# The first down-projection of a transformer block as seven products of quarters, with the context's feed-forward in a phase of its own

## The chip, the cores and the metric

The kernel runs on one core of a Trainium2 chip. A core has a matrix engine (TensorE, called PE in the profile), three engines that work on rows of 128 partitions (VectorE or DVE, ScalarE or ACT, GpSimd or POOL) and a queue (SyncE or SP) that issues the transfers between HBM and the on-chip memory SBUF. PE writes its results to eight accumulation banks of 128 x 512 floats (PSUM), from which ACT or DVE must carry them away. The metric is the time of one execution on the device, in microseconds (us), as the median of several runs.

## The reference, cut to what matters

One layer of a diffusion trunk over 1024 latent tokens and 256 context tokens, 1024 channels each, all in float32. Only the first half of the layer matters here:

```python
def _swiglu(h, w1, w3, w2):
    return (jax.nn.silu(h @ w1) * (h @ w3)) @ w2       # w1, w3: 1024 x 2816, w2: 2816 x 1024

x     = _residual(x,     _swiglu(_modnorm(x,     g[0], m[0],  m[1]),  w1, w3, w2), g[1], m[2],  0.5)
h_ctx = _residual(h_ctx, _swiglu(_modnorm(h_ctx, g[0], mc[0], mc[1]), w1, w3, w2), g[1], mc[2], 0.5)
...   # then projections of both, two attentions, a merge, and a second feed-forward for x alone
def _residual(x, y, g_post, gate, weight):
    return x + weight * gate * _rmsnorm(y, g_post)
```

The product with `w1` and `w3` is the up-projection, the one with `w2` the down-projection. `m` and `mc` are rows of modulation, made from a conditioning vector by nine products with `w_ada`.

## The kernel before, in words

**Three products for one.** PE multiplies float32 numbers that are rounded to a shorter form. To keep the precision every operand is split into a high part (ACT copies it in the short form) and a low part (DVE subtracts the copy from the original); `split` does this, and `mm3` then issues three products: high x high, high x low, low x high.

**Products of quarters.** The up-projection of the latent tokens already saves products: the operands are cut into quarters, and seven products of sums of quarters stand for eight products of quarters. `Unit` is one such set of products for 256 columns of a weight, and makes its sums of weight quarters on DVE. The second feed-forward does the same in its down-projection. There `Gated` stores the gated up-projection (`silu(h w1) * (h w3)`) as seven matrices, three quarters and four sums (`s1` to `s4`, four DVE operations and four stores more for each of the 11 pairs of weight columns, `sums`), and `Quarters` runs 7 x 11 = 77 steps: step n loads one 128 x 512 piece of a matrix (`load_a`, seven steps ahead), splits it and a piece of a weight quarter or of a sum of them (`split`, three steps ahead), and issues four groups of three products into four banks (`product`). The sums of weight quarters (`t1` to `t4`, 44 DVE operations) are made in place by `sum` at steps that `plan` sets. After every eleventh step DVE or ACT takes the four banks out (`out`). The second, third, fifth, sixth and seventh set of eleven steps either go on in the banks of the set ahead, so that PE must not write a bank before it has been read, or start in others.

**The first down-projection is plain.** `Down` takes the 22 row blocks of `w2` in ten groups (nine of two, one of four). For every group it computes ten tiles of 128 tokens x 1024 channels, 0 to 7 the latent tokens, 8 and 9 the context, in two halves, and adds them to `ys` with DVE. Between these tiles stand 44 steps `ctx_up`, the context's up-projection (24 products of 256 columns each). The gated context halves stay in SBUF and enter tiles 8 and 9 as further rows of the same group, with the same split weights.

**The order of the work** is written out by hand. `Plan.step` appends a step of PE work, `Plan.spread` hangs side work (loads, splits, sums) on step numbers, `run` issues step after step. Each engine and the SP queue then works in just this order (`keep_in_program_order`): an instruction that waits holds all behind it. A load of the plan goes into SP's queue at its step; a store, two steps after it was asked for.

**The tail of the phase.** When a tile of `ys` is done, `residual_steps` makes the residual: load of `x` one step ahead (`zero`); at the next step the root of the mean square (ACT squares, POOL takes the power) and, on DVE, a scaling and an addition of 128 x 1024 (`one`, `two`); two and four steps later a second root and a scaling on ACT (`three`, `four`). `plan_chains` puts these at the steps of `pos`. `fill0` then transposes the first four tiles on PE and splits them into the planes for the next projections, whose first product follows at once.

The second down-projection ends in another form of this, `done2`: at its steps 55, 57, 59 and 61 the load of a tile of `x` and a scaling, one step later the addition on DVE and at once (`store(..., 0)`) the store to the output, so that in SP's queue the next tile's load stands behind this store.

**Side work in the same stretch**: `ada_steps(...)` are the modulation products; for each of them DVE adds up 16 scaled pieces of a matrix, or 32 where the context needs its own row (m below 5).

**Buffers**: SBUF pools of 24 tiles `u` and 16 tiles `v` of 128 x 1024, 20 tiles `t` of 128 x 512; PSUM banks `s` (3), `m` (3), `v` (2). The profile names tiles `xu`, `xv`, `t`, `bs`, `bm`, `bv` and all scratch in HBM `d`. Products have line L154 (`mmul`), transposes L157 (`turn_`), all of ACT, DVE and POOL outside attention L120, transfers L132.

Of the kernel before, what the change touches and what calls it, by code (L numbers as in the profile page):

```python
# [43 lines left out]
def hybrid_block(ctx: ExitStack, tc: tile.TileContext, a: dict, out: bass.AP):  # L44
# [25 lines left out]
    def V(dt=F32):  # L70
        return U(dt, "v")
# [313 lines left out]
    def gate_rows(col, key="u"):  # L385
        row = U(key=key)
        for h in range(2):
            pb = PB("s")
# [345 lines left out]
    def up_units(h, w1, w3, gd):  # L734
# [3 lines left out]
        def pair_(p):  # L738
# [6 lines left out]
            def emit3(i, ci, x, bank):  # L745
                y = s.pop((i, ci))
                vec.tensor_tensor(y, x, y, op=ALU.mult)
                if isinstance(gd, Gated):
                    gd.put(p, i, ci, y, units[2 * p + 1].led)
                else:  # L750
                    store(gd[2 * p + i, :, ci * 512:(ci + 1) * 512], y)
# [7 lines left out]

    lap = [0]  # L760

    def PD():
        lap[0] = (lap[0] + 1) % 8
        return PB("smvsmvsm"[lap[0]])

    class Down:


        def __init__(self, w2, gd, ys, fs):
            self.w2, self.gd, self.ys, self.fs = w2, gd, ys, fs  # L770
            self.w, self.g, self.c, self.r = {}, {}, {}, {}

        def loads(self, f, key="v"):
            self.r[f] = load(self.w2[f], key=key), load(self.gd[f], key=key)

        def steps(self, fs=None, key="v"):

            fs = fs or self.fs

            def one(f, e):  # L780
                self.w.setdefault(f, []).append(split(self.r[f][0][:, e * 512:(e + 1) * 512]))

            def two(f):
                self.g[f] = split2(self.r.pop(f)[1])

            s = []
            for f, after in zip(fs, fs[1:] + [None]):
                s += [lambda f=f: one(f, 0), lambda f=f: one(f, 1), lambda f=f: two(f)]
                if after is not None:
                    s[-2] = lambda f=f, n=after: (one(f, 1), self.loads(n, key))  # L790
            return s

        def tile(self, t, es=range(2)):
            ys, fs = self.ys, self.fs
            g = self.g if t < 8 else self.c
            c = slice((t % 8) * P, (t % 8 + 1) * P)
            if fs[0] == 0 and 0 in es:
                ys[t] = V()
            for e in es:
                o = slice(e * 512, (e + 1) * 512)  # L800
                pd = PD()
# [357 lines left out]
    for d in downs:  # L1159
        d.c = cc  # L1160
# [1173 lines left out]
```

## Time and profile before

| what | value |
|---|---|
| median of three runs | 2609.99 us (2607.43 to 2613.73) |
| the profiled execution | 2611.61 us, its span 2609.8 us |
| PE busy | 2576.4 us (99%), 13596 products and transposes |
| DVE, ACT, POOL busy | 1869.2 us (72%), 1189.7 us (46%), 229.4 us (9%) |
| transfers | 433.30 MB, 166 GB/s over the span |
| granted PE clock | 0.997 of full speed |

The span is the time from the first to the last instruction; the execution's own time has 1.8 us more around it. The stages follow each other on PE: up-projection of the latent tokens from 19 to about 455 us, the first down-projection with the context's feed-forward to about 894 us, the projections, the attentions, and from 1871 us the second feed-forward, whose down-projection (in quarters) starts at about 2386 us. In the timelines below the first two columns are the start and the length of a merged group in us, "x6" counts its instructions, and brackets hold the idle time of that engine ahead of the group and what ended it. Instructions of one engine overlap a little: the distance from start to start tells what one costs, not its length.

### The profile page before, as it was taken

Reading aid. Unit: us, or ns where it says so; the run is one execution under the profiler, and the core shown is the slowest. Engines: PE = TensorE matmul, PEld = TensorE weight load, DVE = VectorE, ACT = ScalarE, POOL = GpSimd, SP = SyncE. Lnnn points to the kernel's source line nnn. Section 1 sums busy time; section 2 is a strip of 40 time slices with the busy share of each in tenths; the row PEclk is TensorE's granted clock in tenths of the full one; section 3 lists DMA queues with packets and bytes.
Section 4 is the critical chain, followed back from the end, with each engine's and each line's share of the span. In section 5 each row is a group of like instructions: output and inputs, shape, how many; then the busy total and the mean of one; then the engine's idle time right before and its main releaser. Section 6 shows DMA issues by size and latency. Waiting matters only on the chain.

```text
span 2609.8 us, 37912 instructions
## 1 busy us (share of the span) xinstructions
PE 2576.4 (99%) x13596; PEld 2194.1 (84%) x13596; DVE 1869.2 (72%) x3536; ACT 1189.7 (46%) x2282; POOL 229.4 (9%) x368
## 2 busy tenths in 40 slices
PE   8999999999999999999999999999999999999998
PEld 6888888888888788889889999997788888888886
DVE  4778876587776676775468988886635788766777
ACT  6622223532223663434348987773246322323444
POOL 1000000000000400001003522221021000000003
PEclk9999999999999999999999999999999999999999
DMA  8444433454443575655987742206325444326714
GB/s 303 165 160 142 146 120 117 149 178 149 155 141 114 194 248 175 232 170 173 283 308 268 248 100 74 69 9 223 121 98 192 149 159 167 114 97 239 264 55 174
DMA packets 213501, 433.30 MB, mean 166 GB/s; under 512 B 26880, under 2 KB 68032, under 8 KB 213312
## 3 DMA queue, kind: packets, MB, share of 16 engines
q1 hardware_dynamic: 213312, 430.87, 49.5%
q8 instruction: 107, 1.75, 0.3%
q14 instruction: 82, 0.67, 0.1%
HBM read 318.78 MB, written 112.00 MB: 165 GB/s over the span
## 4 chain that ended last, share of the span: by engine, by line
PE 55%; issue 32%; DVE 6%; ACT 4%; DMA 1%; POOL 1%; SPq 0%; DVEq 0%; ACTq 0%; POOLq 0%
PE bs L154 24%; PE bm L154 16%; PE bv L154 12%; PE bm L157 2%; ACT xu L1914 1%; DVE xu L1778 1%; DVE xv L120 1%; DVE t L1941 1%; ACT t L1940 1%; DVE xu L120 1%; PE bs L157 1%; DVE t L120 1%; POOL st L120 1%; ACT t L1914 0%; ACT t L1754 0%
## 5 line engine op out<-in xcount | busy, mean ns | idle before, releaser
L154 PE MATMUL bm<-xu,xu 128*128 128x512 f32 (+1 forms) x1980 | 469.6, 388 | 1.1 <-ACT t L120 0.8
L154 PEld LDWEIGHTS bm<-xu,xu 128*128 128x128 f32 x1980 | 363.4, 188 | 74.5 <-ACT t L120 2.1
L154 PE MATMUL bs<-xv,xu 128*128 128x512 f32 x1488 | 357.3, 389 | 0.3 <-DVE t L120 0.3
L154 PE MATMUL bv<-xv,xu 128*128 128x512 f32 x1342 | 335.4, 389 | 0.0
L154 PE MATMUL bs<-xu,xu 128*128 128x512 f32 (+1 forms) x1404 | 334.0, 384 | 0.0
L154 PEld LDWEIGHTS bs<-xv,xu 128*128 128x128 f32 x1488 | 279.2, 188 | 58.5 <-issue 0.7
L120 ACT CAST xu<-t 128x512 fp32r<-128x512 f32 x260 | 158.2, 616 | 356.3 <-DVE t L120 355.6
L154 PEld LDWEIGHTS bs<-xu,xu 128*128 128x128 f32 x1404 | 258.0, 188 | 52.0 <-issue 0.8
L154 PEld LDWEIGHTS bv<-xv,xu 128*128 128x128 f32 x1342 | 251.9, 188 | 52.3
L120 DVE TENSOR_TENSOR xu<-t,xu 128x512 fp32r<-128x512 f32 x260 | 178.6, 688 | 127.2 <-ACT xu L120 127.2
L120 DVE TENSOR_TENSOR xu<-xu,xu 128x512 fp32r<-128x512 f32 (+2 forms) x245 | 168.5, 692 | 66.2 <-ACT xu L120 64.6
L120 POOL TENSOR_SCALAR st<-st 128x1 f32<-128x1 f32 (+1 forms) x66 | 42.1, 638 | 1928.0 <-ACT t L120 1917.5
L154 PE MATMUL bs<-w,w 96*128 96x512 f32 (+3 forms) x832 | 206.8, 367 | 2.4 <-DVE st L1803 1.9
L120 DVE TENSOR_TENSOR xu<-xv,xu 128x512 fp32r<-128x512 f32 (+4 forms) x196 | 141.3, 743 | 42.0 <-ACT xu L120 38.8
L154 PE MATMUL bm<-t,xu 128*128 128x256 f32 (+1 forms) x1272 | 165.3, 287 | 0.6 <-ACT t L120 0.4
L154 PEld LDWEIGHTS bm<-t,xu 128*128 128x128 f32 x1272 | 160.7, 191 | 6.0 <-ACT t L120 0.8
L120 ACT ACTIVATE t<-t 128x512 f32<-128x512 f32 (+1 forms) x94 | 57.3, 610 | 223.2 <-DVE t L120 214.2
L120 DVE TENSOR_TENSOR t<-t,t 128x512 f32<-128x512 f32 (+2 forms) x196 | 125.2, 639 | 45.6 <-ACT t L120 42.0
L154 PE MATMUL bv<-t,w 128*128 128x256 f32 x896 | 152.0, 289 | 2.6 <-DVE t L1941 1.9
L154 PEld LDWEIGHTS bv<-t,w 128*128 128x128 f32 x896 | 133.2, 190 | 18.3 <-DVE t L1941 6.8
L120 ACT CAST xu<-xu 128x512 fp32r<-128x512 f32 (+1 forms) x212 | 130.1, 624 | 15.5 <-DMA xu<-in_f1w 8.6
L154 PEld LDWEIGHTS bs<-w,w 96*128 96x128 f32 (+1 forms) x832 | 124.1, 191 | 10.8 <-DVE st L1803 3.3
(225 smaller groups left out, 4126.5 us busy)
## 6 DMA issues: line engine op xcount, KB each, us to landing
d<-t SPq DMA_DIRECT2D x305, 256.0 KB, 2.5
t<-d SPq DMA_DIRECT2D x160, 256.0 KB, 3.4
xv<-in_f1w SPq DMA_DIRECT2D x64, 512.0 KB, 3.6
xu<-in_f1w SPq DMA_DIRECT2D x61, 512.0 KB, 3.8
xu<-in_f2w SPq DMA_DIRECT2D x58, 512.0 KB, 3.6
t<-in_wada SPq DMA_DIRECT2D x112, 256.0 KB, 3.8
xv<-d SPq DMA_DIRECT2D x40, 512.0 KB, 5.8
xu<-in_winT SPq DMA_DIRECT2D x38, 512.0 KB, 4.7
```

Of the source, the lines that this page charges most:

```text
L120: return lambda *x, **y: pin(f(*x, **y))
L154: return pin(nc.tensor.matmul(o, s, m, start=start, stop=stop, skip_group_check=open_group[0]))
L157: return pin(nc.tensor.transpose(o, x, i))
L1778: nc.vector.tensor_scalar(dst, src, 1.0, FMIN, op0=ALU.mult, op1=ALU.max, accum_out=m)
L1914: nc.scalar.activation(x, x, AF.Exp, bias=n_[:, s:s + 1], accum_out=l[:, i:i + 1])
L1940: nc.scalar.copy(t[0], pb)
L1941: nc.vector.tensor_tensor(t[1], pb, f32(t[0]), op=ALU.subtract)
```

## The change

1. The up-projection of the first feed-forward hands its results to a `Gated`, as the second one's does: seven quarters and sums are stored for each pair of weight columns.
2. `Down` and the list of groups are gone. The latent part of the first down-projection is a `Quarters` of 77 steps, right behind the up-projection.
3. The context's feed-forward comes behind it: 44 steps `ctx_up`, then 44 steps `ctx_down`, for which the 22 row blocks of `w2` are loaded and split once more, in halves. Each `ctx_down` issues six products of 512 columns.
4. The residuals of tiles 0 to 3 move into the last third of the 77 steps, those of tiles 4 to 7 to their end and the first steps of `ctx_up`, those of the context tiles into the first steps of the projections. Modulation 4 goes beside the quarters, 3 beside `ctx_up`, 6 to the projections.
5. `fill0` of the first four planes is spread over the second half of `ctx_down`.
6. In `Quarters.plan` the sums of weight quarters get new, mostly earlier steps (and `b22` is loaded two steps earlier). This class is also used by the second down-projection, which so changes too.

```diff
-                for name, first in (("b11", 0), ("b21", NP), ("b12", 9), ("b22", 2 * NP + 4)):
+                for name, first in (("b11", 0), ("b21", NP), ("b12", 9), ("b22", 2 * NP + 2)):
...
-                for name, x in (("t1", 4 + 3 * p // 2), ("t2", 2 * NP + 1 + 3 * p // 2), ("t3", 4 * NP - 4 + p), ("t4", 5 * NP - 3 + p)):
+                for name, x in (("t1", 4 + 4 * p // 3), ("t2", 2 * NP - 1 + 6 * p // 5), ("t3", 3 * NP + p), ("t4", 4 * NP - 1 + p)):
...
-    gd = DR([NF, P, NLAT])
+    gd = Gated()
...
-        store(gd[2 * p, :, 0:512], x)
+        store(gd.d["a11", p], x)
...
+    down1 = Quarters(a["f1w2"], gd, ys)
+    d1_at = down1.plan(plan)
...
+    def ctx_wload(f, e):
+        t = cd[f, e] = T2()
+        ld(t, a["f1w2"][f][:, e * 512:(e + 1) * 512])
+
+    def ctx_wsplit(f, e):
+        cv[f, e] = split(cd.pop((f, e)), key="t")
+
+    def ctx_down(f, e):
+        if f == 0:
+            cb[e] = [PB("vs"[e]) for _ in range(2)]
+        w = cv.pop((f, e))
+        open_group[0] = True
+        for t in range(2):
+            mm3(cb[e][t], [y[:, t * P:(t + 1) * P] for y in cc[f]], w, f == 0, f == NF - 1)
+        open_group[0] = False
+        if f == NF - 1:
+            for t in range(2):
+                if e == 0:
+                    ys[8 + t] = V()
+                act.copy(ys[8 + t][:, e * 512:(e + 1) * 512], cb[e][t])
...
+    o = d1_at + 4 * NP
+    plan.spread(ada_steps((4,)), d1_at + 30, d1_at + 7 * NP - 1)
...
+    e = len(plan.main)
+    plan.spread(first_steps((8, 9), xc, "u"), e - 16, e - 14)
+    plan.spread([m_banks, lambda: normal(xc[0]), lambda: normal(xc[1]), make_hc], e - 12, e - 11)
+    plan.spread([lambda k=k: steps[k]() for k in range(KD)], e - 11, e - 3)
     ups = [(f, x) for f in range(NF) for x in range(2)]
+    up_at = len(plan.main)
+    for f, x in ups:
+        o = len(plan.main)
+        plan.spread([lambda f=f, x=x: ctx_load(f, x)], o - 6, o - 5)
+        plan.spread([lambda f=f, x=x: ctx_split(f, x)], o - 3, o - 2)
+        plan.step(lambda f=f, x=x: ctx_up(f, x))
+    down_at = len(plan.main)
+    for e in range(2):
+        for f in range(NF):
+            o = len(plan.main)
+            plan.spread([lambda f=f, e=e: ctx_wload(f, e)], o - 8, o - 7)
+            plan.spread([lambda f=f, e=e: ctx_wsplit(f, e)], o - 4, o - 3)
+            plan.step(lambda f=f, e=e: ctx_down(f, e))
+    plan.spread(ada_steps((3,)), up_at + 2, down_at - 8)
...
+    for j in range(4):
+        pos[j] = d1_at + 5 * NP + 3 * j
+        pos[4 + j] = up_at - 3 + 3 * j
+    pos[8], pos[9] = len(plan.main) + 1, len(plan.main) + 2
...
-    plan.spread([lead_banks], pos[3] + 3, pos[3] + 4)
-    plan.spread([lambda k=k: fill0s()[k]() for k in range(4)], pos[3] + 6, o)
+    plan.spread([lead_banks], o - 1, o)
+    plan.spread([lambda k=k: fill0s()[k]() for k in range(4)], down_at + NF + 2, o - 1)
     plan.spread([lambda k=k: fill0s()[k]() for k in range(4, KD)], o, o + 2)
...
-    plan.spread(ada_steps((5,)), prest, lat_at - 4)
+    plan.spread(ada_steps((5, 6)), prest, lat_at - 4)
```

Here NF is 22, NP 11, KD 8. The plan's steps are counted from its start: `d1_at` is 155, `up_at` 232, `down_at` 276, and the projections begin at step 320. In the kernel before, the down-projection took steps 155 to 308 and the projections began at 309.

More of the change, by code (lines that the diff above doesn't have):

```diff
@@ L758, in up_units @@
         return units
[L760 to L801, printed above, removed]
-                for x, f in enumerate(fs):
-                    mm3(pd, [y[:, c] for y in g[f]], self.w[f][e], x == 0, x == len(fs) - 1)
-                if fs[0] == 0:
-                    act.copy(ys[t][:, o], pd)
-                else:
-                    vec.tensor_tensor(ys[t][:, o], ys[t][:, o], pd, op=ALU.add)
     class Quarters:
```

100 lines of the change are left out of this document (26 added, 74 removed).

## The prediction

> **What bounds the kernel now.** The page first: PE is busy in 99% of the span, so only what PE executes or waits for can change the time.
>
> ```profile
> PE 2576.4 (99%) x13596; PEld 2194.1 (84%) x13596; DVE 1869.2 (72%) x3536; ACT 1189.7 (46%) x2282; POOL 229.4 (9%) x368
> ```
>
> Next PE's timeline inside the first down-projection, for the price of a product. Groups of six products of 512 columns start 1.36 us apart (561.84 - 560.48), a group of 24 with 256 columns takes 2.87 us (564.71 - 561.84): 0.2267 us and 0.120 us each, with no idle time between.
>
> ```profile
> 560.48 1.52 PE L154 MATMUL bm<-xu,xu 128*128 128x512 f32 x6
> 561.84 3.04 PE L154 MATMUL bm<-t,xu 128*128 128x256 f32 x24
> 564.71 1.55 PE L154 MATMUL bv<-xu,xu 128*128 128x512 f32 x6
> ```
>
> Then the places in the changed stretches where PE does wait. At the context's first up step 24 products take 4.52 us (475.15 - 470.63) and not 2.87: 1.65 us lost on the context's planes.
>
> ```profile
> 470.63 2.39 PE L154 MATMUL bm<-t,xu 128*128 128x256 f32 x18
> 473.44 1.88 PE L154 MATMUL bm<-t,xu 128*128 128x256 f32 x6 [0.42 <-ACT t L120]
> 475.15 1.09 PE L154 MATMUL bs<-xu,xu 128*128 128x512 f32 x4
> ```
>
> At the head of the projections the first 24 products and 16 transposes take 11.72 us (906.03 - 894.31); 24 x 0.2267 and twice the last row's 0.79 would be 7.02: 4.7 us lost, because `fill0` finishes its planes only when they are wanted.
>
> ```profile
> 894.31 1.64 PE L154 MATMUL bm<-xu,t 128*128 128x512 f32 x6
> 896.91 0.50 PE L154 MATMUL bm<-xu,t 128*128 128x512 f32 x1 [0.96 <-DVE xu L120]
> ...
> 899.44 0.97 PE L154 MATMUL bm<-xu,t 128*128 128x512 f32 x2 [0.84 <-DVE xu L120]
> 900.20 1.91 PE L157 MATMUL bs<-ident,xv 128*128 128x128 f32 x8
> 901.76 3.64 PE L154 MATMUL bm<-xu,t 128*128 128x512 f32 x12
> 905.24 1.03 PE L157 MATMUL bs<-ident,xv 128*128 128x128 f32 x8
> 906.03 6.26 PE L154 MATMUL bm<-xu,t 128*128 128x512 f32 x24
> ```
>
> In the second down-projection, where the sixth set of eleven steps hands its banks to the seventh, three steps (each 12 x 0.2267 = 2.72) take 13.09 us (2578.14 - 2565.05) instead of 8.16: 4.9 us lost.
>
> ```profile
> 2565.05 2.23 PE L154 MATMUL bs<-xv,xv 128*128 128x512 f32 x9
> ...
> 2570.99 3.06 PE L154 MATMUL bs<-xv,xv 128*128 128x512 f32 x9 [3.03 <-DVE xv L120]
> ...
> 2575.12 2.50 PE L154 MATMUL bs<-xv,xv 128*128 128x512 f32 x9
> ...
> 2578.14 2.20 PE L154 MATMUL bs<-xv,xv 128*128 128x512 f32 x9
> ```
>
> DVE's and SP's timelines say why. PE waits for DVE to take out the banks (2570.16), and DVE is late: it does sums of weight quarters (2564.97), and waits three times for a tile's load, which SP issues only behind the output store of the tile ahead.
>
> ```profile
> 2559.62 1.28 DVE L120 SCALAR_TENSOR_TENSOR xu<-xu,st,xu 128x1024 f32<-128x1024 f32 x1 [1.40 <-DMA xu<-d]
> ...
> 2564.97 0.69 DVE L120 TENSOR_TENSOR xu<-xu,xu 128x512 f32<-128x512 f32 x1
> 2566.55 1.28 DVE L120 SCALAR_TENSOR_TENSOR xu<-xu,st,xu 128x1024 f32<-128x1024 f32 x1 [0.89 <-DMA xu<-d]
> 2567.75 0.68 DVE L120 TENSOR_TENSOR xv<-t,xv 128x512 fp32r<-128x512 f32 x1
> ...
> 2570.16 1.88 DVE L120 TENSOR_TENSOR xv<-xv,bs 128x512 f32<-128x512 f32 x3
> ```
>
> ```profile
> 2553.49 0.34 SPq L132 DMA_DIRECT2D out_x<-xu  x1
> ...
> 2554.39 0.72 SPq L132 DMA_DIRECT2D xu<-d  x1
> ```
>
> Last the windows: the first up-projection's middle, the second's, the start of the second down-projection, and the loss just shown. The columns are the busy time of PE, its weight loads, DVE, ACT and POOL, then clock, DMA share and GB/s.
>
> ```profile
> 136.00:365.00 229.00, 229.00 (x1012) 189.69 (x1011) 182.83 (x292) 63.05 (x108) 0.00 (x0) 1.00 0.42 143
> 2043.00:2290.00 247.00, 247.00 (x1092) 204.51 (x1091) 189.76 (x300) 70.04 (x122) 0.00 (x0) 1.00 0.44 148
> 2380.00:2430.00 50.00, 50.00 (x222) 41.42 (x221) 37.13 (x62) 20.68 (x37) 0.00 (x0) 1.00 0.94 338
> 2565.00:2580.00 15.00, 11.97 (x46) 9.37 (x46) 14.11 (x24) 8.17 (x18) 5.35 (x1) 0.89 0.84 314
> ```
>
> **The change part by part.** *Products.* Eight latent tiles x 2 halves x 22 rows x 3 = 1056 products of 512 columns become 77 x 4 x 3 = 924. The context keeps its 264 and its 1056 of 256 columns. 132 x 0.2267 = **29.9 us less**, all on the path.
>
> *Gated sums in the first up-projection.* Four DVE operations and three or four more transfers for each pair of units, that is every ten steps. In the 84 steps of the first window these are some 34 operations. What one costs is the distance of two starts, 0.60 us, though it lasts 0.69:
>
> ```profile
> 2519.67 0.69 DVE L120 TENSOR_TENSOR xv<-t,xv 128x512 fp32r<-128x512 f32 x1 [0.83 <-ACT xv L120]
> 2520.28 0.69 DVE L120 TENSOR_TENSOR xv<-xu,xv 128x512 fp32r<-128x512 f32 x1
> ```
>
> DVE goes from 182.8 to about 203 of 229 us. The second up-projection does this already without a PE wait, but at 190 of 247. PE must wait once DVE is more than about a step late with reading a bank. Added up step by step, DVE is never over 1.1 us late (1.0 before). I take 0; the other end is 11 pairs x 4 x 0.6 = 26.
>
> *The 77 steps.* The second down-projection is the same class, and its start shows 50 us with PE full at 338 GB/s. New here is what lies beside its last third: modulation 4 and the residuals. In steps 196 to 219 DVE has 70 operations like those above (42.1 us), 24 scaled additions of the modulation at 0.665 (two take 569.83 - 568.50 = 1.33; 16.0 us), and for four tiles a scaling at 1.20 (2567.75 - 2566.55) and an addition at 1.14 (882.82 - 881.68; 9.4 us): 67.5 us, for 24 x 2.72 + 0.9 of transposes = 66.2 on PE.
>
> ```profile
> 568.50 1.41 DVE L120 SCALAR_TENSOR_TENSOR t<-t,sc,t 128x512 f32<-128x512 f32 x2
> 569.83 0.68 DVE L120 TENSOR_TENSOR xv<-xv,bv 128x512 f32<-128x512 f32 x1
> ...
> 880.36 1.28 DVE L120 SCALAR_TENSOR_TENSOR xv<-xv,st,xv 128x1024 f32<-128x1024 f32 x1 [2.13 <-POOL st L120]
> 881.68 1.23 DVE L120 TENSOR_TENSOR xv<-xv,xv 128x1024 f32<-128x1024 f32 x1
> 882.82 0.68 DVE L120 TENSOR_TENSOR xv<-xv,bs 128x512 f32<-128x512 f32 x1
> ```
>
> Step by step DVE is 3.0 us late at the end of step 219, in just the place where the second down-projection lost its 3.03: the hand-over of banks at 220/221. The reading of the first bank could start 0.68 us into step 220, takes 0.6, and PE wants it 2.04 later than that start: lateness 2.3 + 0.7 for some wait on a load, less 1.4, is 1.6 us of PE wait. Behind it, in step 220, stand the two normalisations of the context's input, which PE transposes at the end of step 221. Counted from the end of step 219, DVE starts at 3.7, reads four banks (2.4), splits (1.2) and scales twice (about 0.7 each), so 8.7; PE is through step 221 at 2 x 2.72 + 1.6 = 7.0: 1.7 more. The clock adds to it: behind the wait of 3.03 it was 0.89 over 15 us, 1.65 us lost; at a chance of 0.4 that is 0.7. Together **4.0 us more**. The bounds: 0 (ACT and POOL early) and 18 (all six roots hold DVE as above, 6 x 2.13, beside this).
>
> The Trainium skill ("TensorE: Matmul & The Clock Gate", HAM oscillation) has the clock halved for a window of 3.4 us once PE idles longer than about 3.4 us. By that rule these waits would cost no clock and the sum would be 0.7 lower. The trace differs: 3.03 us were enough.
>
> *The context's own phase.* Its first up step's 1.65 us go: **1.6 less**; their successor is the wait in step 221, counted above. SP meets a load for up step 236 in step 230 whose buffer PE frees with step 231; all loads behind it wait too. From step 228 to 243, 24 transfers of 512 KB and 7 of 256 KB, 14.4 MB, fall on 45.8 us, 315 GB/s against the 338 shown. A load lands in 3.6 us where the queue is short:
>
> ```profile
> xv<-in_f1w SPq DMA_DIRECT2D x64, 512.0 KB, 3.6
> xu<-in_f2w SPq DMA_DIRECT2D x44, 256.0 KB, 5.4
> ```
>
> The one for step 236 has four steps, 11.5 us, from its issue, less ACT's and DVE's split of some 2.3. I take **1.0 more** for the queue, between 0 and 6. In `ctx_down` a step takes 6 x 0.2267 = 1.36 us on PE and 0.6 on DVE; its 256 KB (193 GB/s) is asked for eight steps, 10.9 us, ahead, and the slowest row is 5.4. I take 0; without that cover it would be up to 44 x 0.5.
>
> *Head of the projections.* The first four planes are now made in steps 298 to 319, long before. The last four still come at 320 to 322, beside the context's residuals. Of 4.7 us I take **3.7 less**; between 0 and 4.7. The first weights have 6 x 1.36 = 8.2 us from load to use, where landing (3.6) and split (about 1.3) need 4.9.
>
> *Second down-projection.* The last eleven sums move from steps 52 to 62 to 43 to 53, out of the late stretch: DVE has 8 operations, 4.8 us, less between steps 55 and 65. But load behind store is a loop: from one scaling to the next 6.93 us (2566.55 - 2559.62), where two steps are 5.44. It starts about 2 us earlier now, so the wait of 3.03 falls to about 1.0, and the half clock with it: **3.5 less** of 4.9, between 0 and 4.9.
>
> *Moved at no cost:* modulation 6 goes to the projections (16 DVE operations in 75 steps), the second `w2` load is in the transfers above.
>
> **Sum:** -29.9 + 4.0 - 1.6 + 1.0 - 3.7 - 3.5 = -33.7. From the profiled 2611.6 that is 2577.9. The median shown, 2610.0, lies 1.6 lower, so **2577 us**, a little towards the median.
>
> **The rivals.**
> - *Only the products count.* The two heads keep their losses (the store-load loop speaks for it, the early planes against): 2577 + 7 = 2584.
> - *DVE is held by the roots.* In the kernel before each residual holds DVE 2.13 us, while POOL makes the root. Six of these in steps 209 to 220 without slack are 12.8, tiles 4 to 7 add some 4: 2577 + 15 = 2592. Against it: tiles 1 to 3 are complete before their step, so ACT and POOL can be early.
> - *The gated sums tip the first up-projection*: up to 26 us, most of it 20: 2597. Against it: no bank is read more than 1.1 us late.
> - *Slower: the context's phase runs at the pace of its loads.* If buffers hold SP all along, so that one load is in flight, an up step takes 3.6 + 2.3 = 5.9 instead of 2.87, 44 x 3.0 = 133 us: 2710. It decides from 0.8 us in each up step (34 / 44). For it speaks the block at step 230, against it that loads stand six steps ahead, with buffers free from step 232.
>
> **How the numbers follow.** Forecast 0.58 (its own range 2570 to 2583), only the products 0.18, roots 0.14, sums 0.05, slower 0.05. The range 2567 to 2593 takes in the first three. All but the last are faster by over 0.2%, which is about what a measurement of this kernel can tell from no change: 0.94 faster, 0.02 the same, 0.04 slower.
>
> **What would show it.** Right: 13464 products, PE without waits of over 0.3 us from 40 to 390 us and in the context's two phases; waits on DVE near 635 us of together 2 to 5 us; the head of the projections within 1.5 us of its sum; the wait near the end about 1 us. Wrong: a DVE row with a POOL wait in each residual, PE waiting for DVE in the first up-projection, or ACT waiting for DMA at every up step.

## The result and the profile after

The changed kernel takes 2596.26 us (2595.78 to 2597.27, four runs); the kernel before took 2608.77 us beside it. The ratio is 0.9949, with a 95% interval of 0.9932 to 0.9966: faster by half a per cent, where the prediction had 2577 us, 1.3% faster. The direction is right, the size about two fifths. The number lies outside the range of 2567 to 2593.

The profiled execution took 2596.1 us, its span is 2594.3 us, 15.5 us shorter than before. The busy times of the page, after:

```profile
PE 2548.6 (98%) x13464; PEld 2166.9 (84%) x13464; DVE 1885.7 (73%) x3552; ACT 1246.2 (48%) x2362; POOL 224.3 (9%) x368
```

The 132 products are gone (13596 to 13464). But PE's busy time fell by 27.8 us and the span by only 15.5: PE waits 12.3 us more than before. (What a step loses is here always the distance from its first product to that of the next step, less its products at 0.2267 us for 512 columns and 0.120 for 256.) The losses stand in four places.

*In the first up-projection.* The window of the prediction, and PE's waits from 130 to 400 us (which engine's instruction ended them; us in total, times, longest):

```profile
136.00:365.00 229.00, 223.03 (x971) 180.81 (x971) 192.00 (x310) 59.87 (x103) 0.00 (x0) 1.00 0.49 170
```

```profile
PE bs L154 <- DVE t L120: 6.8, 10, 1.3
```

Before, the same window had 229.00 us of PE and 1012 products; now 41 products fewer fit in, which is 9.3 us; with one more wait, at 379.89, PE loses 10.7 us from 203 to 400 us. PE waits ten times for DVE, though DVE has 37 us without work. How that can be is seen around the wait at 264.53, first on PE, then on DVE and ACT:

```profile
260.55 2.88 PE L154 MATMUL bv<-xv,xu 128*128 128x512 f32 x12
264.53 2.99 PE L154 MATMUL bs<-xv,xu 128*128 128x512 f32 x12 [1.10 <-DVE t L120]
```

```profile
256.77 0.68 DVE L120 TENSOR_TENSOR t<-t,bv 128x512 f32<-128x512 f32 x1
258.66 0.69 DVE L120 TENSOR_TENSOR xu<-t,xu 128x512 fp32r<-128x512 f32 x1 [1.21 <-ACT xu L120]
...
261.76 0.69 DVE L120 TENSOR_TENSOR xu<-t,xu 128x512 fp32r<-128x512 f32 x1 [1.21 <-ACT xu L120]
262.37 1.41 DVE L120 SCALAR_TENSOR_TENSOR t<-t,sc,t 128x512 f32<-128x512 f32 x2
263.69 0.68 DVE L120 TENSOR_TENSOR t<-bs,t 128x512 f32<-128x512 f32 x1
```

```profile
257.49 0.63 ACT L120 ACTIVATE t<-t 128x512 f32<-128x512 f32 x1 [1.96 <-DVE t L120]
258.03 0.60 ACT L120 CAST xu<-t 128x512 fp32r<-128x512 f32 x1
```

DVE and ACT wait for each other in turn. DVE completes a block (256.77), ACT applies its function (257.49) and makes, behind it in its queue, the high part of a weight (258.03); DVE's next instruction is the low part of that weight (258.66) and waits 1.21 us for it, with everything else of DVE behind it. While ACT does its two operations DVE stands still, and while DVE works ACT stands still (1.96 us ahead of 257.49 in the change's trace). So the pair of scaled additions (262.37) comes late, and the reading of bank `bs` (263.69) for which PE waits comes later still.

These waits are not new. Over the same window DVE's waits for the high part of a weight are nearly the same, first in the kernel before, then in the change (us in total, times, longest):

```profile
DVE xu L120 <- ACT xu L120: 33.1, 34, 1.2
DVE xu L120 <- ACT xu L120: 31.4, 32, 1.2
```

Before, 182.8 us of work and 33.1 of such waits make 215.9 of 229, and DVE has the rest free. In the change 192.0 and 31.4 make 223.4 for only 971 products; for 1012 that would be some 233 us, more than the window has. This is an estimate from these rows; it takes the waits to grow with the products.

*At the hand-over of banks in steps 220 and 221*, PE and DVE:

```profile
643.52 2.20 PE L154 MATMUL bs<-xv,xv 128*128 128x512 f32 x9
...
650.83 4.18 PE L154 MATMUL bs<-xv,xv 128*128 128x512 f32 x9 [4.43 <-DVE xv L120]
654.81 1.48 PE L154 MATMUL bm<-xv,xv 128*128 128x512 f32 x3
...
656.30 2.29 PE L154 MATMUL bs<-xv,xv 128*128 128x512 f32 x9
```

```profile
645.70 1.41 DVE L120 SCALAR_TENSOR_TENSOR t<-t,sc,t 128x512 f32<-128x512 f32 x2
647.54 1.28 DVE L120 SCALAR_TENSOR_TENSOR xv<-xv,st,xu 128x1024 f32<-128x1024 f32 x1 [0.44 <-POOL st L120]
648.86 1.23 DVE L120 TENSOR_TENSOR xv<-xv,xu 128x1024 f32<-128x1024 f32 x1
650.00 1.88 DVE L120 TENSOR_TENSOR xv<-xv,bs 128x512 f32<-128x512 f32 x3
```

Two steps and two transposes, 5.65 us of work, take 12.78 (656.30 - 643.52): 7.1 lost, 4.6 of it waiting and 2.5 at about half the clock (nine products take 3.98 us, 654.81 - 650.83, instead of 2.04; the granted clock is 0.50 from 649.5 to 656.1 us). DVE reads the first bank at 650.00, 5.8 us after it could (643.52 + 0.68); ahead of it stand a modulation's pair, a wait for the root and the residual.

*In the context's first up steps*, 236 to 242:

```profile
699.22 8.89 PE L154 MATMUL bm<-t,xu 128*128 128x256 f32 x72 [0.50 <-DVE xu L120]
708.87 3.14 PE L154 MATMUL bm<-t,xu 128*128 128x256 f32 x24 [0.76 <-DVE xu L120]
712.65 5.77 PE L154 MATMUL bm<-t,xu 128*128 128x256 f32 x46 [0.64 <-DVE xu L120]
720.02 0.51 PE L154 MATMUL bm<-t,xu 128*128 128x256 f32 x2 [1.60 <-ACT xu L120]
721.28 13.90 PE L154 MATMUL bm<-t,xu 128*128 128x256 f32 x102 [0.75 <-DVE xu L120]
```

```profile
705.13 1.29 DVE L120 SCALAR_TENSOR_TENSOR xv<-xv,st,xu 128x1024 f32<-128x1024 f32 x1 [0.74 <-POOL st L120]
706.46 1.22 DVE L120 TENSOR_TENSOR xv<-xv,xv 128x1024 f32<-128x1024 f32 x1
707.60 1.22 DVE L120 TENSOR_TENSOR xu<-xv,xu 128x1024 fp32r<-128x1024 f32 x1
```

Step by step 6.9 us are lost here: the 144 products from 699.22 to 721.28 take 22.06 us for 17.3 of work, and the rest lies ahead of 699.22 and in slower products behind 721.28 (the granted clock is 0.50 from 721.1 to 724.4 us, which costs some 1.6). The weights' low part that PE wants at 708.87 is made at 707.60, behind a residual's two operations and its wait for the root.

*In the projections*, beside modulation 6, three steps lose 2.2 us together; the row is one of the three:

```profile
1032.03 2.99 PE L154 MATMUL bs<-xv,xu 128*128 128x512 f32 x12 [0.81 <-DVE t L120]
```

And the gains. At the head of the projections the first 24 products and 16 transposes take 7.14 us (892.74 - 885.60), before 11.72; in the second down-projection two steps across the hand-over take 5.88 us (2559.65 - 2553.77) for 5.44 of work:

```profile
885.60 2.89 PE L154 MATMUL bm<-xu,t 128*128 128x512 f32 x12
...
892.74 6.27 PE L154 MATMUL bm<-xu,t 128*128 128x512 f32 x24
```

```profile
2553.77 2.20 PE L154 MATMUL bs<-xv,xv 128*128 128x512 f32 x9
...
2556.83 2.30 PE L154 MATMUL bs<-xv,xv 128*128 128x512 f32 x9 [0.18 <-DVE xv L120]
...
2559.65 2.20 PE L154 MATMUL bs<-xv,xv 128*128 128x512 f32 x9
```

The terms, in us of the span:

| place | forecast | measured |
|---|---|---|
| products | -29.9 | -29.9 |
| gated sums, first up-projection | 0 | +10.7 |
| hand-over in the 77 steps | +4.0 | +7.1 |
| context's first up step | -1.6 | -2.2 |
| context's up steps 236 to 242 | +1.0 | +6.9 |
| head of the projections | -3.7 | -4.6 |
| modulation 6 in the projections | 0 | +2.2 |
| second down-projection | -3.5 | -4.6 |
| sum | -33.7 | -14.4 |

(The row of the first up step contains a second wait of 0.6 us, at step 185 of the kernel before, which went too. The span fell by 15.5, so 1.1 us more went outside these places; about 1.0 of it is a stretch at half the clock that the profile of the kernel before has from 1384.5 to 1387.8 us, with a granted clock of 0.50, and that of the change has not.)

### The profile page after: what moved, and what is told of

Its sections match the earlier page's. It is cut to its first block, busy times and chain, and to the rows that moved or that the text cites. A ratio compares the mean times of both kernels' runs of the same rounds, so it can differ in the third digit from the quotient of the medians.

```text
span 2594.3 us, 38254 instructions
## 1 busy us (share of the span) xinstructions
PE 2548.6 (98%) x13464; PEld 2166.9 (84%) x13464; DVE 1885.7 (73%) x3552; ACT 1246.2 (48%) x2362; POOL 224.3 (9%) x368
## 4 chain that ended last, share of the span: by engine, by line
PE 61%; issue 25%; DVE 7%; ACT 5%; DMA 1%; POOL 1%; SPq 0%; DVEq 0%; ACTq 0%; POOLq 0%
PE bs L154 25%; PE bm L154 20%; PE bv L154 12%; PE bm L157 2%; DVE t L120 2%; DVE xu L120 1%; ACT xu L1862 1%; DVE xv L120 1%; DVE xu L1726 1%; DVE t L1889 1%; ACT t L1888 1%; ACT xu L120 1%; PE bs L157 1%; POOL st L120 1%; ACT t L120 1%
## 5 line engine op out<-in xcount | busy, mean ns | idle before, releaser
L154 PE MATMUL bm<-xu,xu 128*128 128x512 f32 (+2 forms) x1584 | 368.8, 387 | 1.0 <-ACT t L120 0.9
L120 ACT CAST xu<-t 128x512 fp32r<-128x512 f32 (+1 forms) x282 | 167.1, 599 | 421.9 <-DVE t L120 405.3
L120 DVE TENSOR_TENSOR xu<-t,xu 128x512 fp32r<-128x512 f32 (+1 forms) x282 | 187.9, 667 | 137.9 <-ACT xu L120 137.9
L154 PE MATMUL bs<-xv,xv 128*128 128x512 f32 x1014 | 250.6, 393 | 4.6 <-DVE xv L120 4.6
L154 PE MATMUL bs<-xu,xu 128*128 128x512 f32 (+1 forms) x1008 | 234.2, 382 | 0.6 <-DVE t L120 0.6
L120 DVE TENSOR_TENSOR xu<-xu,xu 128x512 fp32r<-128x512 f32 (+1 forms) x272 | 185.5, 688 | 60.3 <-ACT xu L120 59.9
L154 PEld LDWEIGHTS bs<-xv,xv 128*128 128x128 f32 x1014 | 190.6, 189 | 44.6 <-issue 5.4
L154 PEld LDWEIGHTS bs<-xu,xu 128*128 128x128 f32 x1008 | 184.1, 188 | 38.2 <-issue 2.2
L120 ACT CAST xv<-t 128x512 fp32r<-128x512 f32 x154 | 95.7, 621 | 151.9 <-PE bv L154 65.5
L154 PE MATMUL bm<-xv,xv 128*128 128x512 f32 x618 | 165.1, 391 | 0.0
```

The costliest lines, as they stand in the source:

```text
L120: return lambda *x, **y: pin(f(*x, **y))
L154: return pin(nc.tensor.matmul(o, s, m, start=start, stop=stop, skip_group_check=open_group[0]))
```

## The experiments

Every experiment is the changed kernel with one or a few steps of the plan moved, except where it says otherwise. Times are medians of four runs (before_sums: ten) beside the kernel before on the same chip. Most intervals are some 0.3% or 8 us wide, mostly because the kernel before scatters (2607 to 2614 us); so what an experiment did to one place is read from its trace, and times that differ by less than 3 us decide little by themselves.

| run | us | ratio to before, interval |
|---|---|---|
| the change | 2596.26 | 0.9949, 0.9932 to 0.9966 |
| mod2_in_down | 2586.90 | 0.9911, 0.9897 to 0.9926 |
| mod4_early | 2590.45 | 0.9927, 0.9912 to 0.9941 |
| store_late | 2595.72 | 0.9948, 0.9933 to 0.9962 |
| mod3_late | 2598.00 | 0.9955, 0.9938 to 0.9971 |
| resid_apart | 2597.53 | 0.9946, 0.9931 to 0.9961 |
| root_ahead | 2594.50 | 0.9936, 0.9921 to 0.9950 |
| before_sums | 2607.22 | 0.9987, 0.9978 to 0.9997 |
| mod6_late | 2596.51 | 0.9944, 0.9929 to 0.9959 |
| resid_down | 2594.62 | 0.9946, 0.9931 to 0.9961 |
| planes_late | 2597.49 | 0.9954, 0.9938 to 0.9971 |
| all_moved | 2586.85 | 0.9915, 0.9900 to 0.9929 |
| moved3 | 2578.15 | 0.9871, 0.9857 to 0.9886 |
| moved2a | 2579.16 | 0.9876, 0.9860 to 0.9892 |

### Modulation 2 out of the first up-projection (mod2_in_down)

```diff
-    plan.spread(ada_steps((2,)), rest1 + 10, len(plan.main) - 10)
+    plan.spread(ada_steps((2,), "s"), d1_at + 2, d1_at + 44)
```

The `"s"` puts the modulation's own sum on PE into a bank of another pool.

> Only modulation 2 moves: from the first up-projection to steps 157 to 198 of the first down-projection (41 steps, 32 scaled additions, 21 us of DVE). In the changed kernel PE loses 9.4 us between steps 63 and 123 (203 to 380 us), nearly all behind DVE. Theory: modulation and gated sums together take DVE's slack there, and the stores and reloads of the sums cost nothing. Then these waits fall below 1 us and the time goes 8 to 9 us down, to some 2587, if the first down-projection, where DVE is busy 11 to 16 of 20 us, takes the modulation for nothing. Rival: the sums alone do it, by their place in the order between DVE and ACT or by their loads on SP: then 6 us or more stay and the time is 2593 to 2596.

Measured: 2586.9 us, 9.4 less than the change. PE has no listed wait between 130 and 400 us any more, and the window is full:

```profile
136.00:365.00 229.00, 229.00 (x1012) 189.69 (x1011) 183.28 (x293) 63.06 (x108) 0.00 (x0) 1.00 0.47 162
```

With the kernel before this makes three of four cases. Modulation alone (before): DVE 182.8 us, no wait. Sums alone (here): 183.3 us, no wait. Both (the change): the 10.7 us (the 9.4 of the expectation leave out the wait at 379.89). So neither the sums' place in the queues nor their transfers cost anything by themselves; the theory stands. DVE's waits for ACT are there with the sums alone too (33.4 us, 34 times), and fit. Steps 157 to 198 of the down-projection took the modulation for the 1.1 us that PE loses wherever a modulation's own sum stands.

### Modulation 4 earlier in the first down-projection (mod4_early)

```diff
-    plan.spread(ada_steps((4,)), d1_at + 30, d1_at + 7 * NP - 1)
+    plan.spread(ada_steps((4,), "s"), d1_at + 2, d1_at + 44)
```

> Only modulation 4 moves: from steps 185 to 231 of the first down-projection to steps 157 to 198. Between 643 and 656 us (steps 220 and 221, the hand-over of banks) the changed kernel loses 7.1 us. Theory: the 16 us of modulation beside steps 196 to 219 make DVE 5.8 us late; without them it is not late, the loss falls below 2.5 us (what the context's two normalisations leave) and the wait of 1.1 us for the modulation's bank at step 225 goes; some 5 to 6 us down, to 2590 to 2591. Rival: the residuals' own chain (ACT, POOL, DVE, with DVE held by the roots) makes DVE late: 5 us or more stay, 2595 to 2596.

Measured: 2590.45 us, 5.8 less than the change. The hand-over loses 0.8 us instead of 7.1; the stretch from 640 to 660 us, first in the change, then here:

```profile
640.00:660.00 20.00, 15.57 (x60) 12.27 (x59) 16.98 (x26) 11.85 (x22) 9.44 (x10) 0.83 0.46 160
```

```profile
640.00:660.00 20.00, 19.58 (x89) 15.72 (x88) 15.52 (x25) 15.45 (x29) 5.22 (x10) 1.00 0.41 144
```

The rival, that the residuals alone make DVE late, falls: the same residuals stand there with 0.8 us of loss (0.6 in all_moved below, which has no modulation there either). The clock's drop went with the wait.

### The first roots a step ahead (root_ahead)

```diff
-            for x, f in zip((-1, 0, 0, slot, 2 * slot), chains(t)):
+            for x, f in zip((-2, -1, 0, slot, 2 * slot) if max(at) == 9 and t < 8 else (-1, 0, 0, slot, 2 * slot), chains(t)):
```

> Only the first root of each of the eight residuals moves, and the load of the tile with it: one step ahead of the residual, so that POOL can be done before DVE comes to it. Theory that the roots hold DVE: four waits of 0.4 to 0.7 us ahead of the hand-over at steps 220 and 221 and four of 0.74 in the context's up steps go; the loss of 7.1 us at the hand-over falls to 4 to 5 and that of 6.9 at steps 236 to 242 to 3 to 5, 4 to 6 us together, 2590 to 2592. Rival (DVE's own work, and its turns with ACT, fill these steps with or without the roots): both losses change by less than 1 us, 2595 to 2597.

Measured: 2594.5 us, 1.8 less than the change. The wait at the hand-over, 4.43 us in the change, is 2.59, and the two steps lose 4.2:

```profile
650.63 2.89 PE L154 MATMUL bs<-xv,xv 128*128 128x512 f32 x9 [2.59 <-DVE xv L120]
653.32 1.48 PE L154 MATMUL bm<-xv,xv 128*128 128x512 f32 x3
```

In the up steps 236 to 242 still 6.3 are lost. The theory fits the hand-over and fails for the up steps. Some of it is scatter: in kernels that leave this place alone the hand-over lost between 4.9 and 7.1 us. That moved3 below, with the same step and again a wait of 2.59, lost 4.1 speaks for an effect of 1 to 3 us. The up steps scatter too: without a change to them they lost 5.3 in mod6_late and 7.1 in mod2_in_down.

### The context's up steps: four tries

The stores later (store_late):

```diff
-                                           after=(lambda: store(dst, ys[t])) if t < 8 else None))
+                                           after=(lambda: store(dst, ys[t], 7)) if t < 8 else None))
```

> Only the stores of the eight residual tiles move: they are issued 7 steps behind their residual instead of 2. In the context's first up steps (236 to 242, 698 to 725 us) the changed kernel loses 6.9 us. Theory: SP stands at such a store until DVE has made the tile, and holds the weight loads behind it (SP issues nothing for 7 us three times there). Then the 6.9 us fall below 3 and the time goes 4 to 6 us down, to 2590 to 2592. Rival: DVE is late by its own work there (residuals, modulation 3, splits of weights), whatever SP does: the loss stays at 5 to 7 us and the time at 2595 to 2597.

Modulation 3 later (mod3_late):

```diff
-    plan.spread(ada_steps((3,)), up_at + 2, down_at - 8)
+    plan.spread(ada_steps((3,)), up_at + 14, down_at)
```

> Only modulation 3 moves: its first loads and scaled additions are at step 246 instead of 234, so that none lies beside the context's up steps 236 to 242. Theory of the held stores: the loss of 6.9 us there stays above 5, and the time at 2594 to 2597. Rival (DVE late by its own work): four to five pairs of scaled additions, 5 to 7 us of DVE, are gone from that stretch, and the loss falls below 3 us, the time to 2590 to 2592.

The residuals of tiles 4 to 7 eight steps apart (resid_apart) and in the down steps (resid_down):

```diff
-        pos[4 + j] = up_at - 3 + 3 * j
+        pos[4 + j] = up_at + 9 + 8 * j     # resid_apart
+        pos[4 + j] = down_at + 3 + 5 * j   # resid_down
```

> Only the residuals of tiles 4 to 7 move: to steps 241, 249, 257 and 265, eight apart, instead of 229, 232, 235 and 238. The stores behind them go along. Theory: in the context's up steps a residual's two operations (2.4 us of DVE, 0.74 us of waiting for the root) and its two squares and one scaling on ACT stand in both queues ahead of the split of the next weights, and each engine then waits for the other; no engine alone is full. Then the 6.9 us of steps 236 to 242 fall below 1.5, the late residuals cost below 2 us together, and the time goes 4 to 6 us down, to 2590 to 2592. Rival: the burst of weight loads behind the block of SP at step 230 makes the weights late. The block stays, so 4 us or more stay, at 2594 to 2597.

> Only the residuals of tiles 4 to 7 move, into the context's down steps: 279, 284, 289 and 294. Eight steps apart in the up steps, beside modulation 3, they cost 8.1 us, as much as three apart. Theory: an up step with modulation 3 leaves DVE and ACT too little beside their waits for each other; a residual anywhere in it costs some 2 us. A down step needs 0.6 us of DVE in 1.36, so there the residuals cost below 1 us together, nothing is lost from step 236 to 275 but the 1 us of the modulation's own bank, and the time goes 5 to 7 us down, to 2589 to 2591. Rival: a residual's hold of DVE costs its 2 us wherever it stands; then 6 us or more are lost between 279 and 300 and the time is 2595 to 2597.

The later stores left 6.4 of the 6.9 us: the held store, my first explanation, is not the cause. Without modulation 3 beside these steps 5.8 were left, and 1.7 more were lost at steps 266 and 270, where modulation 3 now stood closer: my second explanation, DVE's sheer work, fell too. Eight steps apart, the residuals left the up steps 236 to 242 without loss, but each took its loss along: 8.1 us between 246 and 261. PE's waits from 690 to 780 us there:

```profile
PE bm L154 <- DVE xu L120: 5.9, 7, 1.5
```

So the burst of loads behind SP's block is not the cause either: it was still there. With the residuals in the down steps the up steps are free (only the 1 us of the modulation's own sum is lost between 236 and 275), as the theory said, but 4.5 us are lost at 294 and 299, more than it allowed: 2594.6 us. DVE shows why, in the last of the four:

```profile
845.84 1.28 DVE L120 SCALAR_TENSOR_TENSOR xv<-xv,st,xu 128x1024 f32<-128x1024 f32 x1 [1.28 <-POOL st L120]
848.11 1.23 DVE L120 TENSOR_TENSOR xv<-xv,xv 128x1024 f32<-128x1024 f32 x1 [0.99 <-DMA xv<-in_x]
```

A residual's lead is counted in steps, and a down step has 1.36 us, so that the root and the tile come too late. What follows: in an up step the cause is the residual beside the splits, with and without modulation 3. That the DVE-ACT turns make it so is read from the rows; no run separates them from the residual's own work. Neither engine is full: DVE 25.1 and ACT 20.9 of 32 us:

```profile
698.00:730.00 32.00, 27.74 (x212) 26.72 (x211) 25.09 (x32) 20.91 (x32) 4.01 (x10) 0.95 0.86 323
```

Residuals eight steps apart without modulation 3 weren't tried.

### The new steps of the quarter sums alone (before_sums)

```diff
-                for name, first in (("b11", 0), ("b21", NP), ("b12", 9), ("b22", 2 * NP + 4)):
+                for name, first in (("b11", 0), ("b21", NP), ("b12", 9), ("b22", 2 * NP + 2)):
...
-                for name, x in (("t1", 4 + 3 * p // 2), ("t2", 2 * NP + 1 + 3 * p // 2), ("t3", 4 * NP - 4 + p), ("t4", 5 * NP - 3 + p)):
+                for name, x in (("t1", 4 + 4 * p // 3), ("t2", 2 * NP - 1 + 6 * p // 5), ("t3", 3 * NP + p), ("t4", 4 * NP - 1 + p)):
```

This is the kernel before with these two lines.

> The kernel before, with the new steps of the quarter sums in its second down-projection and nothing else. Forecast: of the 4.9 us lost at the hand-over of the sixth set to the seventh 3.5 go, with about 1 us of wait left. In the changed kernel 4.6 were gone. If the sums' steps alone do it, 4 to 5 us go and the time is 0.15 to 0.19% below the kernel before (about 2605). Rival: the changed placement of all that stands ahead moved the loads and stores against each other there, and the sums' steps do little: less than 2 us.

Measured: 2607.22 us, a ratio of 0.9987 (3.4 us). Three steps across the hand-over take 8.97 us (2572.64 - 2563.67) where they took 13.09:

```profile
2563.67 2.20 PE L154 MATMUL bs<-xv,xv 128*128 128x512 f32 x9
...
2567.11 2.29 PE L154 MATMUL bs<-xv,xv 128*128 128x512 f32 x9 [0.56 <-DVE xv L120]
...
2572.64 2.20 PE L154 MATMUL bs<-xv,xv 128*128 128x512 f32 x9
```

4.1 of the 4.6 us come from these two lines alone; which of the two, no run tells.

### The early planes undone (planes_late)

```diff
-    plan.spread([lambda k=k: fill0s()[k]() for k in range(4)], down_at + NF + 2, o - 1)
+    plan.spread([lambda k=k: fill0s()[k]() for k in range(4)], o - 4, o)
```

> Only the first four planes of the projections move back: to the last four steps ahead of the projections, about where the kernel before made them. The head of the projections loses 1.5 us in the changed kernel and lost 4.7 to 6 before. If the early planes are what won this, the loss comes back to 4 to 5.5 us and the time goes up to 2599 to 2600. Rival: it went because the latents' last residuals no longer stand there; then the loss stays below 2.5 us and the time at 2596 to 2597.

Measured: 2597.49 us. The first 24 products and 16 transposes of the projections take 8.05 us (892.90 - 884.85), 0.9 more than in the change:

```profile
884.85 2.85 PE L154 MATMUL bm<-xu,t 128*128 128x512 f32 x10
...
892.90 3.29 PE L154 MATMUL bm<-xu,t 128*128 128x512 f32 x11
```

The rival was right. Of the 4.6 us won at the head, the early planes are 0.9; by elimination the rest came with the residuals of the eight latent tiles, which no longer stand in the last steps ahead of it. That part is argued from this run, not shown by one of its own.

### Modulation 6 behind the attention (mod6_late)

```diff
-    plan.spread(ada_steps((5, 6)), prest, lat_at - 4)
+    plan.spread(ada_steps((5,)), prest, lat_at - 4)
...
-    plan.spread(ada_steps((7,)), 2, len(plan.main) - 4)
+    plan.spread(ada_steps((6, 7)), 2, len(plan.main) - 4)
```

> Only modulation 6 moves: out of the projections, to stand ahead of modulation 7 in the stage behind the attention. In the changed kernel the projections lose 2.2 us at steps 370, 375 and 380 (1028 to 1060 us), which the kernel before did not. If its 16 scaled additions and 16 loads cause this, all of it goes, 2594 us; the stage that takes it has DVE slack and pays below 0.5. Rival: these waits come from the other work's new place against the loads there, and stay: 2596.

Measured: 2596.51 us, the same as the change. The projections' 2.2 us went, as expected, but the stage that took the modulation lost 4.9 us more, 3.4 of them in four waits that it did not have.:

```profile
PE bm L154 <- ACT xu L120: 3.4, 4, 1.2
```

The forecast that this stage has room was wrong: it is only 32 steps long, and two modulations in 26 of them leave none. The time did not rise because the hand-over and the up steps, which this run leaves alone, happened to lose 3.1 us less in its profile (5.7 and 5.3).

### Everything moved (all_moved), and what was too much

```diff
-    plan.spread(ada_steps((2,)), rest1 + 10, len(plan.main) - 10)
-    plan.spread(ada_steps((4,)), d1_at + 30, d1_at + 7 * NP - 1)
+    plan.spread(ada_steps((2,), "s"), d1_at + 2, d1_at + 43)
+    plan.spread(ada_steps((4,), "s"), d1_at + 3, d1_at + 44)
+    plan.spread(ada_steps((6,)), down_at + 22, down_at + 43)
-        pos[4 + j] = up_at - 3 + 3 * j
+        pos[4 + j] = down_at + 3 + 5 * j
-    plan.spread(ada_steps((5, 6)), prest, lat_at - 4)
+    plan.spread(ada_steps((5,)), prest, lat_at - 4)
```

and the line of root_ahead.

> All placements that lost time, moved together: modulations 2 and 4 beside steps 157 to 199 of the first down-projection, residuals of tiles 4 to 7 in the context's down steps, the residuals' first roots a step ahead, modulation 6 in the context's last down steps. If each loss has the cause found alone, 9.4 + 6 + 6 + 2 = 23 us go, less 1 to 2 us for the modulations' banks: 2574 to 2576, what the prediction had for the change. If the first down-projection can't take two modulations (43 us of DVE where some 55 are free), it loses 3 to 8 us again: 2577 to 2583.

Measured: 2586.85 us. Two modulations beside steps 157 to 199 don't fit. PE's waits from 500 to 600 us:

```profile
PE bm L154 <- DVE xv L120: 7.5, 3, 6.0
```

From step 176 to 189, 14 us are lost, the longest wait at a hand-over of banks again. DVE had room for one modulation there (mod2_in_down), and the 43 us of work that "some 55 free" would have held did not fit: from 500 to 560 us DVE works without a pause, 60 of 60 us. Why the room ahead of that was left unused (16.4 of 20 us busy from 480 to 500) is not shown.

This run also tells the two moves of the next kernel apart. Its residuals are still five steps apart, but with the root and the load a step earlier no root and no load holds DVE, and the loss at 294 and 299 is 1.3 us where resid_down has 4.5, although modulation 6 begins there too. So the earlier root and load are worth some 3 us, the greater distance the rest.

### The kernel that reaches the forecast (moved3, moved2a)

moved3 has the first two lines below and the line of root_ahead; moved2a has besides the others:

```diff
-    plan.spread(ada_steps((2,)), rest1 + 10, len(plan.main) - 10)
+    plan.spread(ada_steps((2,), "s"), d1_at + 2, d1_at + 44)
-        pos[4 + j] = up_at - 3 + 3 * j
+        pos[4 + j] = down_at + 4 + 10 * j
# moved2a alone:
-    plan.spread(ada_steps((4,)), d1_at + 30, d1_at + 7 * NP - 1)
+    plan.spread(ada_steps((4,)), d1_at + 45, d1_at + 7 * NP + 14)
-    plan.spread(ada_steps((3,)), up_at + 2, down_at - 8)
+    plan.spread(ada_steps((3,), "s"), up_at + 14, down_at + 14)
```

> Three moves together: modulation 2 into steps 157 to 198 of the first down-projection, modulation 4 where the change has it, the residuals of tiles 4 to 7 ten steps apart in the context's down steps (280, 290, 300, 310), each first root a step ahead of its residual and the tile's load two steps. If causes add: 9.4 from the first up-projection, 2.9 of the 7.1 at the hand-over, and of the 6.9 in the up steps all but 1: 18 us down, 2577 to 2580. The residuals five apart lost 4.5 us at steps 294 and 299, where DVE waited 0.95 to 1.41 us for each root and 0.39 to 0.99 for the tile's load. If these waits were it, ten apart and a step earlier cost below 1 us. Rival: two normalisations' work on ACT is too much for steps of 1.36 us at any distance; 3 us or more stay and the time is 2581 to 2584.

> As the run with modulation 2, the roots and the residuals of tiles 4 to 7 moved, and besides modulation 4 at steps 200 to 245 instead of 185 to 231, modulation 3 at 246 to 289 instead of 234 to 267. Theory of the hand-over: DVE's lateness is gathered in steps 196 to 219; with some 8 scaled additions less there (5 us) the loss at 220 and 221 falls from 4 to below 2, and the time to 2575 to 2578. Rival: modulations beside steps 209 to 219 and the context's transposes do it, at the same density as before: the loss stays at 3 to 5, and modulation 3 costs 1 to 4 us in the down steps: 2579 to 2583.

moved3 took 2578.15 us, 1.3% below the kernel before and 18.1 below the change, as worked out (18; by the two ratios, each beside the kernel before on its own chip, it is 20). The residuals ten steps apart with roots and loads ahead cost nothing: no root holds DVE any more, and of the loads one does, for 0.59 us ahead of the first. The third of the four:

```profile
838.41 1.28 DVE L120 SCALAR_TENSOR_TENSOR xv<-xv,st,xu 128x1024 f32<-128x1024 f32 x1
839.72 1.23 DVE L120 TENSOR_TENSOR xv<-xv,xv 128x1024 f32<-128x1024 f32 x1
```

PE's waits from 660 to 860 us are one of 0.7 us, which the change has too:

```profile
PE bs L157 <- ACT xv L120: 0.7, 1, 0.7
```

So the waits were most of the price of a residual in the down steps, and the rival (ACT too full at any distance) falls. moved2a did not improve on it, with 2579.16 us: the hand-over still lost 4.2 us, now mostly at the context's transposes, and modulation 3 lost 3.2 in the down steps, its own sum included. Of its two theories the second is the better. The loss at the hand-over needs a modulation in reach of it, wherever the lateness began; that it needs the residuals as well is argued, since no run has the modulation there without them. The best median of the study is that of moved3, with moved2a inside its interval; moved3's hand-over still loses 4.1 and its projections 2.2.

## Why the prediction was right or wrong, point by point

*Products*: right, 13464, and 29.9 us.

*Gated sums in the first up-projection*: wrong, and the largest error, 10.7 us. The step that failed is "Added up step by step, DVE is never over 1.1 us late". The prediction holds DVE's own work, some 203 of 229 us, against PE's and has no term for DVE's waits for ACT in the middle of its queue, up to 1.21 us at a time. The trace of the kernel before had them, 33.1 us in the window: 203 + 33 is 236, more than 229. The second up-projection, which was taken as the model, has the sums but no modulation; mod2_in_down shows that this was the difference. As a rival it stood in the text at 0.05, with the right row to look for and, by accident of the other terms, nearly the right time (2597, with a loss of 20 us here instead of 10.7).

*The 77 steps*: place and mechanism right, mis-sized at 7.1 for 4.0. The term "lateness 2.3 + 0.7 for some wait on a load" measured 5.8 (DVE's first reading at 650.00). The roots, which the sum held at nothing and the second rival at 2.13 each, are part of the difference: root_ahead's wait is 1.8 us shorter. The clock cost 2.5 where 0.7 was taken. The 1.7 for the context's normalisations didn't show in the change, where DVE had caught up during the long wait; mod4_early has 0.8 of it.

*The context's own phase*: the old loss went (2.2 for 1.6). The 1.0 for SP's queue named the wrong resource. The up steps lost 6.9, and neither the queue nor the stores did it (store_late, resid_apart, and moved3, where SP's block at step 230 remained and the up steps lost nothing). The sum had the residuals of tiles 4 to 7 under no term there. The second rival gave them "some 4", by the roots; the roots are 0.6 of it, which is within the scatter. Some 1.6 of the 6.9 is clock, for which the sum had no term there either. `ctx_down` at nothing was right.

*Head of the projections*: size right (4.6 for 3.7, within its bounds), partly by luck, for the reason given was mostly wrong: the early planes are 0.9 of it.

*Second down-projection*: right in place and sign, 4.6 for 3.5, and in cause as far as before_sums goes, with 4.1 from the two lines alone. The wait left, 0.18 us, is below the 1 us expected.

*Moved at no cost*: modulation 6 cost 2.2 in the projections. It was put at 16 operations in 75 steps; it looks like the up-projection's error again, a modulation beside DVE-ACT turns: ahead of the wait at 1032.03 DVE is held twice for 1.30 us by ACT. That the modulation is needed for the loss mod6_late shows, the rest is argued.

*Only the products count* and *the context's phase at the pace of its loads* did not happen: the heads lost their waits, and no up step lost more than 2.5 us.

## What to carry to other kernels

Where two engines hand each other work in the order of their queues, add up the turns, not the work of each: here DVE at 84% and ACT at 26% of a window together held PE for 9.3 us of it. The waits of one for the other can be read off the kernel before. A cover that has been seen to hold one piece of side work says nothing of two: the losses of this change came where a second thing was put beside a first that just fitted (modulation and sums, modulation and residuals, residual and weight splits). And count the lead of a load or a root in microseconds: a load one step ahead came in time where a step has 2.88 us, and up to 0.99 us late where it has 1.36.

## What the runs showed of the hardware

The granted clock fell after shorter waits than the 3.03 us of the kernel before, but the length of one wait does not decide it. Behind the 2.59 us of root_ahead nine products took 2.69 us (653.32 - 650.63) instead of 2.04, and the granted clock is 0.50 from 652.2 to 655.5 us. Behind a wait of the same 2.59 us at the same place in moved3 they took 2.16 (640.95 - 638.79), near full speed:

```profile
638.79 2.32 PE L154 MATMUL bs<-xv,xv 128*128 128x512 f32 x9 [2.59 <-DVE xv L120]
640.95 0.84 PE L154 MATMUL bm<-xv,xv 128*128 128x512 f32 x3
```

In resid_down, behind 2.25 us, eleven took 2.63, which is also near full speed (2.49):

```profile
850.00 2.80 PE L154 MATMUL bs<-t,xu 128*128 128x512 f32 x11 [2.25 <-DVE t L120]
852.63 0.60 PE L157 MATMUL bm<-ident,xu 128*128 128x128 f32 x4
```

And in the change's up steps the clock fell behind two waits of 1.60 and 0.75 us, 1.26 us apart from start to start (720.02 and 721.28), with shorter ones ahead of them. The Trainium skill ("TensorE: Matmul & The Clock Gate", HAM oscillation) puts the fall behind a gap above some 3.4 us; here it came behind less, once behind 2.59 us and another time not. What decides it, these rows don't tell.

For 40 us of the first down-projection of the change, 480 to 520, the transfers reached more than the 338 GB/s of the prediction, 390 and then 386, with no PE wait beside them:

```profile
480.00:500.00 20.00, 20.00 (x90) 16.57 (x89) 9.11 (x16) 8.27 (x15) 0.00 (x0) 1.00 1.05 390
```
